# A decoder trunk in fp32: gated projections that begin with half of the rows, loads from two queues, and later sums for the first norm

## Chip, cores, metric

One Trainium2 chip, one core. The metric is device time of the whole program in microseconds, the median of several executions. Each run shown has also one profiled execution, and the tables below are of that one.

## What is computed

Two layers, each a half-step gated FFN, a mixer of three kinds of attention, and a second half-step gated FFN, on 256 tokens of width 1024; a norm stands ahead of each part and at the end.

```python
def _rmsnorm(x, g):
    y = x * lax.rsqrt(jnp.mean(x * x, axis=-1, keepdims=True) + RMS_EPS)
    return y * g

def _swiglu(x, w_gate, w_up, w_down):          # 1024 -> 2816 -> 1024
    return (jax.nn.silu(x @ w_gate) * (x @ w_up)) @ w_down

for l in range(DEPTH):                          # DEPTH = 2
    x = x + 0.5 * _swiglu(_rmsnorm(x, ffn1_norm[l]), ffn1_w_gate[l], ffn1_w_up[l], ffn1_w_down[l])
    h = _rmsnorm(x, mix_norm[l])
    ...                                         # out_a, out_b, out_c from h @ w_in[l]
    x = x + jnp.concatenate([out_a, out_b, out_c], axis=-1) @ w_out[l]
    x = x + 0.5 * _swiglu(_rmsnorm(x, ffn2_norm[l]), ffn2_w_gate[l], ffn2_w_up[l], ffn2_w_down[l])
return _rmsnorm(x, final_norm)
```

## The kernel before

Activations lie transposed: eight row tiles x[k] of 128 features by 256 tokens. All products are in fp32 by halves. A weight chunk of 128 x 1024 is loaded raw, ACT casts its high half (`whi`, line 152) and DVE subtracts to get the low half (`wlo`, line 153); an operand tile is likewise made of a high half, times the norm's gain, on ACT (line 229) and a low half on DVE (line 230). `mm2` (line 284) makes one pair of matmuls: the high weights times both halves of the operand (512 columns), then the low weights times the high half (256 columns).

In an FFN (line 302) the 2816 columns of gate and up go in 22 steps of 128. Column i needs two chunks: (i, 0) holds the weights of gate and up for rows 0 to 3, (i, 1) those for rows 4 to 7, so each chunk is eight pairs. The chunks are computed in the order (0, 0), (0, 1), (1, 0), (1, 1), (2, 0), (2, 1), and then column by column. A column needs two PSUM banks, of the tag "mm" (four banks), or "at" (four banks) for each third column. `next_w` hands out chunks in the order in which they are loaded and splits the chunk three further on, except at two places of the head, whose splits are made up for after `norm.column()`.

The norm's scale is applied late. `square` (line 233) takes the squares of two row tiles on ACT and adds them on GpSimd (lines 243, 247); `column` multiplies the sums by ones on TensorE (`pss`) and takes the power on GpSimd; `rms_row` turns the result into a row on TensorE (`prow`). Where this is done in the head of an FFN is said by `AT`: the column after pair 33, the row after pair 42 of 48. Then each column is evacuated (`add_halves`, line 295), scaled, put through Silu on ACT, multiplied, and split into halves for the down projection.

At the start of the program the SP queue issues, one after the other: the gains, row tile 0, the weights for it, row tiles 1 to 3, the weights for them, row tiles 4 to 7, the second chunk, and then further chunks (lines 175 to 186). GpSimd makes an identity, and TensorE runs 12 warm-up products on it (24 matmuls; line 217). Lines 710 to 718 make the operands of all eight row tiles and the halves of the first three chunks; the squares of the first norm come after the first two chunks of products. The order on each engine is that of a list scheduler, which follows the order of the program where inputs are ready; TensorE's order is the program's.

Of the kernel before, what the change touches and what calls it, by code (L numbers as in the profile page):

```python
# [10 lines left out]
F32 = mybir.dt.float32  # L11
F32R = mybir.dt.float32r
AF = mybir.ActivationFunctionType
OP = mybir.AluOpType

P = 128
# [3 lines left out]
DK = D // P  # L20
# [15 lines left out]
NDIST = 384  # L36
CH = DK * P
RAW, SPLIT_AHEAD = 5, 3
WARM = 12
AT = (0, 9)  # L40

FIRST = ((0, 1), (1, 4))

# [34 lines left out]
def tile_trunk(ctx, tc, xT, gains, kvg, sinks, table, onehot, wgu, wdn, winv, wins, wkv, wout, out):  # L78
# [47 lines left out]
    def room(i):  # L126
        raws[i] = wpool.tile([P, 2, CH], F32, tag="raw", name=f"raw{i}", bufs=RAW)
        return raws[i]
# [33 lines left out]
    def next_w(pieces=1, ahead=True):  # L162
        n = cursor[0]
        cursor[0] += 1
        split(n)
        if ahead:
            split(n + SPLIT_AHEAD, pieces)
        load(n + 2 * RAW - 1)
        return parts.pop(n)
# [2 lines left out]
    xs = act.tile([P, DK, T], F32, name="xs")  # L172
    x = [xs[:, k, :] for k in range(DK)]
    gain = const.tile([P, (3 * DEPTH + 1) * DK], F32, name="gain")
    nc.sync.dma_start(out=gain, in_=gains)
    room(0)
    for a, b in FIRST:
        nc.sync.dma_start(out=xs[:, a:b, :], in_=xT[:, a:b, :])
        nc.sync.dma_start(out=raws[0][:, 0, 2 * a * P:2 * b * P], in_=loads[0][:, 0, 2 * a * P:2 * b * P])
    nc.sync.dma_start(out=xs[:, DK // 2:, :], in_=xT[:, DK // 2:, :])  # L180
    nc.sync.dma_start(out=raws[0][:, 1, :], in_=loads[0][:, 1, :])
    room(1)
    for j in range(2):
        nc.sync.dma_start(out=raws[1][:, j, :], in_=loads[1][:, j, :])
    for n in range(2, RAW):
# [5 lines left out]
    nc.gpsimd.memset(ident, 0.0)  # L191
    nc.gpsimd.affine_select(out=ident, in_=ident, pattern=[[-1, P]], compare_op=OP.not_equal,
                            fill=1.0, base=0, channel_multiplier=1)
    ones = const.tile([P, 1], F32, name="ones")
    nc.vector.memset(ones, 1.0)
    mhalf = const.tile([P, 2], F32, name="mhalf")
    nc.vector.memset(mhalf, -0.5)

# [100 lines left out]
        nc.vector.tensor_add(a, p[:, :T], b)  # L299
        return a  # L300

    def ffn(norm, nxt, last=False, first=None, between=(), at=AT):
        hs, banks, ws = [], {}, {}

        def products(i, h, start=0, stop=DK):

            if start == 0:
                ws[0] = next_w(ahead=(i, h) not in ((1, 1), (2, 0)))
                if h == 0:
                    for m in range(2):  # L310
                        banks[i, m] = bank("pgu", "at" if i % 3 == 2 else "mm")
            whi, wlo = ws[0]
            for j in range(start, stop):
                k, m = h * DK // 2 + j // 2, j % 2
                c = slice(j * P, (j + 1) * P)
                mm2(banks[i, m], whi[:, c], wlo[:, c], xx[k], k == 0, k == DK - 1)


        products(0, 0)
        products(0, 1)  # L320
        if first:
            first()
        products(1, 0)
        products(1, 1)
        for n in range(2 * DK):
            products(2, n // DK, n % DK, n % DK + 1)
            if n == at[0]:
                col = norm.column()
                for m in range(2):
                    split(cursor[0] + SPLIT_AHEAD - 2 + m)  # L330
            if n == at[1]:
                row = rms_row(col)
        for i in range(FK):
            if i in between:
                between[i]()
            if i > 2:
                products(i, 0)
                products(i, 1)
            g, u = add_halves(banks.pop((i, 0)), "A"), add_halves(banks.pop((i, 1)), "C")
            t = tmp.tile([P, T], F32, tag="A", name="t")  # L340
            nc.vector.tensor_mul(t, g, row)
            s = tmp.tile([P, T], F32, tag="B", name="s")
            nc.scalar.activation(s, t, AF.Silu)  # L343
            sr = tmp.tile([P, T], F32, tag="B", name="sr")
            nc.gpsimd.tensor_mul(sr, s, row)  # L345
            h = tmp.tile([P, T], F32, tag="h", name="h", bufs=2)
            nc.vector.tensor_mul(h, sr, u)  # L347
            hs.append(act.tile([P, 2, T], F32R, tag=("hh", "hl")[i % 2], name=f"h{i}", bufs=FK // 2))
            nc.scalar.copy(hs[i][:, 0, :], h)  # L349
            nc.vector.tensor_sub(hs[i][:, 1, :], h, f(hs[i][:, 0, :]))  # L350
        for k in range(DK):
            p = bank("pdn")
            for kk in range(FK):
                j = (k * FK + kk) % DK
                if j == 0:
                    whi, wlo = next_w()
                c = slice(j * P, (j + 1) * P)
                mm2(p, whi[:, c], wlo[:, c], hs[kk], kk == 0, kk == FK - 1)
            if last and k:
                turn(k - 1)  # L360
            nc.vector.scalar_tensor_tensor(x[k], p[:, T:], 0.5, x[k], op0=OP.mult, op1=OP.add)
            residual(k, k + 1, p[:, None, :T], 0.5, nxt, last)
            nxt.square(k, last)
            if last:
                ys[k] = tmp.tile([P, T], F32, tag="A", name="y")
                nc.scalar.activation(ys[k], x[k], AF.Copy, scale=nxt.g(k))
# [342 lines left out]

    norm = Norm(0)  # L710
    parts[0], parts[1] = halves_of(0), halves_of(1)
    for k in range(DK):
        norm.operands(k)
        if k < DK // 2:
            split_part(0, 2 * k * P, 2 * (k + 1) * P)
        elif k % 2:
            split_part(1, (k - 5) * 2 * P, (k - 3) * 2 * P)
    split(2)
    start = norm

    def first_squares():
        for k in range(DK):
            start.square(k, after=start.ops[0])

    for l in range(DEPTH):
        nxt = Norm(3 * l + 1)
        ffn(norm, nxt, first=first_squares if l == 0 else None, between={3: load_bias, 6: make_bias} if l == 0 else {})
        norm, nxt = nxt, Norm(3 * l + 2)
        mix(l, norm, nxt)
        norm, nxt = nxt, Norm(3 * l + 3)  # L730
        ffn(norm, nxt, last=l == DEPTH - 1)
        norm = nxt
# [34 lines left out]
def _layout(x, rel_bias_table, ffn1_norm, ffn1_w_gate, ffn1_w_up, ffn1_w_down, mix_norm, w_in, attn_sinks,  # L767
            kv_norm_c, w_kv_up_c, w_out, ffn2_norm, ffn2_w_gate, ffn2_w_up, ffn2_w_down, final_norm):
    def cols(w, tiles):

        r = _rows(w)
        *a, p, k, n = r.shape
        return np.moveaxis(r.reshape(*a, p, k, tiles, n // tiles), -2, -4)

    g = np.stack([v for l in range(DEPTH) for v in (ffn1_norm[l], mix_norm[l], ffn2_norm[l])] + [final_norm])
    gu, dn = [], []
    for l in range(DEPTH):
        for wg, wu, wd in ((ffn1_w_gate, ffn1_w_up, ffn1_w_down), (ffn2_w_gate, ffn2_w_up, ffn2_w_down)):
            c = np.stack([cols(wg[l], FK), cols(wu[l], FK)], axis=3).reshape(FK, P, 2, DK * P)
            gu.append(np.moveaxis(c, 2, 1).reshape(2 * FK, P, DK * P))  # L780
            c = cols(wd[l], DK).reshape(DK, P, FK, P).transpose(0, 2, 1, 3).reshape(FK, DK, P, P)
            dn.append(np.moveaxis(c, 1, 2).reshape(FK, P, DK * P))
    order = [c for _, hs in STAT for h in hs for c in range(h, h + HD)]
    vcol = list(range(_VA, _VA + 128)) + list(range(_VB, _VB + 256)) + list(range(_WI, _WI + 4))
    rv = _rows(w_in[:, :, vcol])
    winv = np.moveaxis(rv.reshape(DEPTH, P, 4, 2 * VCOLS), 2, 1)
    wins = cols(w_in[:, :, order], NST).reshape(DEPTH, NST, P, DK * P)
    wkv = np.concatenate([w_kv_up_c[:, :, :HD], w_kv_up_c[:, :, :HD], w_kv_up_c[:, :, HD:]], axis=2)
    wo = w_out.reshape(DEPTH, NH, HD, D)[:, HEADS].reshape(DEPTH, DK, P, D)
    last = wo[:, -LASTK:].reshape(DEPTH, LASTK, P, DK, P).transpose(0, 3, 1, 2, 4).reshape(DEPTH, LASTK, DK, P, P)  # L790
    wo[:, -LASTK:] = last.transpose(0, 1, 3, 2, 4).reshape(DEPTH, LASTK, P, D)
    return {
        "xT": np.moveaxis(x[0].T.reshape(DK, P, T), 0, 1),
        "gains": np.moveaxis(g.reshape(-1, DK, P), 2, 0).reshape(P, -1),
        "kvg": kv_norm_c.T,
        "sinks": attn_sinks[:, HEADS[:NA]].reshape(1, -1),
        "table": rel_bias_table,
        "onehot": _distances(),
        "wgu": np.stack(gu),
        "wdn": np.stack(dn),  # L800
        "winv": winv,
        "wins": wins,
        "wkv": wkv,
        "wout": wo,
    }
# [17 lines left out]
```

## Time and profile before

| | |
|---|---|
| median of 3 runs | 972.26 us (971.99 to 973.49) |
| profiled execution, whole | 975.89 us |
| its span, first to last instruction | 974.1 us |
| TensorE busy | 955.7 us, 98% of the span |
| VectorE (DVE) busy | 706.3 us, 73% |
| ScalarE (ACT) busy | 533.8 us, 55% |
| GpSimd (POOL) busy | 161.6 us, 17% |
| DMA | 174.41 MB, mean 179 GB/s |

Times of instructions are from the start of the span. A row of the timeline gives start, duration, engine (PE is TensorE; a q behind the name is the engine's queue), line, operation, the tile written and those read, and in brackets the idle time before it with what ended it. Ends of matmuls are modelled, so distances are better taken from start to start.

### The profile page before, as it was taken

What the parts mean: (1) busy time and instruction counts of PE and PEld (TensorE: products, weight loads), DVE (VectorE), ACT (ScalarE), POOL (GpSimd) and SP (SyncE); (2) the same over time, 40 slices, a digit from 0 to 9 for tenths busy, and PEclk for the clock granted to TensorE, in tenths of its full rate; (3) what the DMA queues carried; (4) which work ended last, traced back from release to release, by engine and by line L of the source; (5) the groups of instructions that cost most, each with busy time, mean ns of one, the idle gap of its engine ahead of it and who ended that gap; (6) DMA issues with size and microseconds to landing.
All of it is one profiled execution on the core that took longest, in us unless ns stands there. A gap on an engine that the chain in (4) does not pass through costs nothing.

```text
span 974.1 us, 15598 instructions
## 1 busy us (share of the span) xinstructions
PE 955.7 (98%) x5924; PEld 846.5 (87%) x5924; DVE 706.3 (73%) x1307; ACT 533.8 (55%) x960; POOL 161.6 (17%) x148
## 2 busy tenths in 40 slices
PE   8999999999999999999999999999999999999996
PEld 6888888898899888888888888889988988888885
DVE  5787775668956877776668777666797678777552
ACT  6655554444656665654446555544465576555442
POOL 3221110110102221110012121001002042121001
PEclk9999999999999999999999999999999999999998
DMA  8688545553334555555555555545433455556511
GB/s 335 217 302 297 199 173 184 181 187 112 121 131 135 196 192 197 189 175 190 196 173 181 208 174 197 192 158 210 152 131 95 166 173 179 209 174 194 196 44 43
DMA packets 47575, 174.41 MB, mean 179 GB/s; under 512 B 3291, under 2 KB 5867, under 8 KB 47372
## 3 DMA queue, kind: packets, MB, share of 16 engines
q1 hardware_dynamic: 47212, 172.90, 51.8%
q8 instruction: 46, 0.75, 0.3%
q10 hardware_dynamic: 288, 0.52, 0.1%
q14 instruction: 29, 0.24, 0.1%
HBM read 172.34 MB, written 4.22 MB: 181 GB/s over the span
## 4 chain that ended last, share of the span: by engine, by line
PE 89%; DVE 4%; issue 4%; ACT 1%; POOL 1%; DMA 1%; SPq 0%; POOLq 0%; DVEq 0%; ACTq 0%
PE pgu L210 49%; PE pdn L210 22%; PE pp L210 6%; PE pwo L210 5%; PE pv L210 2%; PE po L210 1%; PE psc L210 1%; PE pt L213 1%; DVE wlo L153 1%; POOL ss L243 1%; DVE acc L494 1%; ACT whi L152 1%; DMA raw<-wgu 1%; DVE m L493 1%; DVE sb L565 0%
## 5 line engine op out<-in xcount | busy, mean ns | idle before, releaser
L210 PE MATMUL pgu<-xx,whi 128*128 128x512 f32 x1408 | 494.6, 396 | 2.0 <-ACT whi L152 2.0
L153 DVE TENSOR_TENSOR wlo<-raw,whi 128x1024 fp32r<-128x1024 f32 (+2 forms) x322 | 392.9, 1223 | 135.2 <-ACT whi L152 127.7
L152 ACT CAST whi<-raw 128x1024 fp32r<-128x1024 f32 (+2 forms) x322 | 332.7, 1034 | 257.6 <-PE pdn L210 110.1
L210 PE MATMUL pgu<-xx,wlo 128*128 128x256 f32 x1408 | 395.0, 281 | 0.2 <-DVE wlo L153 0.2
L210 PEld LDWEIGHTS pgu<-xx,whi 128*128 128x128 f32 x1408 | 264.0, 188 | 64.4 <-ACT whi L152 2.7
L210 PEld LDWEIGHTS pgu<-xx,wlo 128*128 128x128 f32 x1408 | 266.1, 189 | 0.8 <-DVE wlo L153 0.8
L210 PE MATMUL pdn<-h,whi 128*128 128x512 f32 x704 | 248.2, 397 | 0.0
L210 PE MATMUL pdn<-h,wlo 128*128 128x256 f32 x704 | 197.6, 281 | 0.0
L210 PEld LDWEIGHTS pdn<-h,whi 128*128 128x128 f32 x704 | 132.1, 188 | 31.3
L345 POOL TENSOR_TENSOR sr<-s,rrow 128x256 f32<-128x256 f32 x88 | 98.1, 1115 | 355.1 <-ACT s L343 354.8
L210 PEld LDWEIGHTS pdn<-h,wlo 128*128 128x128 f32 x704 | 133.1, 189 | 0.0
L297 ACT COPY b<-pgu 128x256 f32<-128x256 f32 x176 | 65.3, 372 | 80.8 <-PE pgu L210 80.8
L210 PE MATMUL pp<-xx,whi 128*128 128x256 f32 x480 | 92.1, 292 | 0.0
L299 DVE TENSOR_TENSOR a<-pgu,b 128x256 f32<-128x256 f32 x176 | 73.5, 419 | 25.3 <-ACT b L297 24.8
L210 PEld LDWEIGHTS pp<-xx,whi 128*128 128x128 f32 x480 | 75.4, 194 | 2.7 <-issue 1.7
L210 PE MATMUL pp<-xx,wlo 128*128 128x256 f32 x240 | 68.2, 284 | 0.0
L347 DVE TENSOR_TENSOR h<-sr,a 128x256 f32<-128x256 f32 x88 | 37.4, 425 | 29.2 <-POOL sr L345 28.8
L210 PE MATMUL pwo<-ohl,whi 128*128 128x256 f32 x256 | 47.6, 287 | 0.0
L210 PEld LDWEIGHTS pp<-xx,wlo 128*128 128x128 f32 x240 | 46.5, 194 | 0.0
L349 ACT CAST h<-h 128x256 fp32r<-128x256 f32 x88 | 35.3, 401 | 18.6 <-DVE h L347 18.6
L243 POOL TENSOR_TENSOR ss<-sq 128x512 f32<-128x512 f32 x7 | 10.2, 1458 | 196.4 <-ACT sq L238 196.4
L571 ACT ACTIVATE e<-sb,nm 128x256 f32<-128x256 f32 x64 | 28.4, 446 | 25.8 <-DVE nm L565 25.8
(98 smaller groups left out, 692.1 us busy)
## 6 DMA issues: line engine op xcount, KB each, us to landing
raw<-wgu SPq DMA_DIRECT2D x86, 1024.0 KB, 5.0
raw<-wdn SPq DMA_DIRECT2D x44, 1024.0 KB, 4.9
raw<-wins SPq DMA_DIRECT2D x14, 1024.0 KB, 5.0
raw<-wout SPq DMA_DIRECT2D x8, 1024.0 KB, 4.9
raw<-winv SPq DMA_DIRECT2D x4, 776.0 KB, 4.2
w<-u SPq DMA_DIRECT2D x1, 3072.0 KB, 14.1
bias<-w SPq DMA_DIRECT2D x1, 2048.0 KB, 9.3
raw<-wgu SPq DMA_DIRECT2D x3, 512.0 KB, 7.9
```

The lines of the kernel that those rows point to most:

```text
L152: ops = (nc.scalar.copy(hi[:, a:b], raw(n, a, b)), nc.vector.tensor_sub(lo[:, a:b], raw(n, a, b), f(hi[:, a:b])))
L153: nc.vector.tensor_sub(lo[:, a:b], raw(n, a, b), f(hi[:, a:b])))
L210: in_order(nc.tensor.matmul(*a, **kw))
L213: in_order(nc.tensor.transpose(*a))
L243: nc.gpsimd.tensor_add(s, self.sums[0], sq)
L297: nc.scalar.copy(b, p[:, T:])
L299: nc.vector.tensor_add(a, p[:, :T], b)
L345: nc.gpsimd.tensor_mul(sr, s, row)
L347: nc.vector.tensor_mul(h, sr, u)
L349: nc.scalar.copy(hs[i][:, 0, :], h)
L493: nc.vector.max(out=m8, in_=acc[:, cs])
L571: nc.scalar.activation(e[:, cs], sb[:, cs], AF.Exp, scale=-1.0, bias=nms[i][:, b, m:m + 1], accum_out=dens[i][:, b, m:m + 1])
```

## The change

Chunks of the first three columns are computed and laid out in memory in the order (0, 0), (1, 0), (2, 0), (0, 1), (1, 1), (2, 1), in all four FFNs. The first column's banks are evacuated after the fourth of them. In the first FFN the norm's column stands after pair 38 and its row after pair 48; in the others after 33 and 42, as before. At the start, rows 0 to 3 go out from SP, and the weights for them, the gains, and rows 4 to 7 from ACT's queue. A Silu of one element on ACT, between the first and the second weight load, brings the function table. The operands of rows 4 to 7 come after the split of the second chunk, and the squares of the first norm are set among the operands and splits, ahead of the FFN. There are 9 warm-up products in place of 12.

```diff
-WARM = 12
-AT = (0, 9)
+WARM = 9
+HEAD = ((0, 0), (1, 0), (2, 0), (0, 1), (1, 1), (2, 1))
+AT = ((4, 0), (5, 1))
+AT0 = ((4, 5), (5, 7))
...
-    nc.sync.dma_start(out=gain, in_=gains)
+    ones = const.tile([P, 1], F32, name="ones")
+    nc.vector.memset(ones, 1.0)
     room(0)
-    for a, b in FIRST:
+    for i, (a, b) in enumerate(FIRST):
         nc.sync.dma_start(out=xs[:, a:b, :], in_=xT[:, a:b, :])
-        nc.sync.dma_start(out=raws[0][:, 0, 2 * a * P:2 * b * P], in_=loads[0][:, 0, 2 * a * P:2 * b * P])
-    nc.sync.dma_start(out=xs[:, DK // 2:, :], in_=xT[:, DK // 2:, :])
+        nc.scalar.dma_start(out=raws[0][:, 0, 2 * a * P:2 * b * P], in_=loads[0][:, 0, 2 * a * P:2 * b * P])
+        if i == 0:
+            nc.scalar.dma_start(out=gain, in_=gains)
+            nc.scalar.activation(tmp.tile([P, 1], F32, tag="first", name="first", bufs=1), ones, AF.Silu)
     nc.sync.dma_start(out=raws[0][:, 1, :], in_=loads[0][:, 1, :])
+    nc.scalar.dma_start(out=xs[:, DK // 2:, :], in_=xT[:, DK // 2:, :])
     room(1)
...
-        products(0, 0)
-        products(0, 1)
-        if first:
-            first()
-        products(1, 0)
-        products(1, 1)
-        for n in range(2 * DK):
-            products(2, n // DK, n % DK, n % DK + 1)
-            if n == at[0]:
-                col = norm.column()
-                for m in range(2):
-                    split(cursor[0] + SPLIT_AHEAD - 2 + m)
-            if n == at[1]:
-                row = rms_row(col)
+        done = {}
+        for n, (i, h) in enumerate(HEAD):
+            for j in range(DK):
+                products(i, h, n not in (at[0][0] - 1, at[0][0]), j, j + 1)
+                if (n, j) == at[0]:
+                    col = norm.column()
+                    for m in range(2):
+                        split(cursor[0] + SPLIT_AHEAD - 2 + m)
+                if (n, j) == at[1]:
+                    row = rms_row(col)
+            if (i, h) == (0, 1):
+                done[0] = gate_and_up(0)
...
-            g, u = add_halves(banks.pop((i, 0)), "A"), add_halves(banks.pop((i, 1)), "C")
+            g, u = done.pop(i, None) or gate_and_up(i)
...
-    for k in range(DK):
+    for k in range(DK // 2):
         norm.operands(k)
-        if k < DK // 2:
-            split_part(0, 2 * k * P, 2 * (k + 1) * P)
-        elif k % 2:
-            split_part(1, (k - 5) * 2 * P, (k - 3) * 2 * P)
-    split(2)
-    start = norm
-
-    def first_squares():
-        for k in range(DK):
-            start.square(k, after=start.ops[0])
+        split_part(0, 2 * k * P, 2 * (k + 1) * P)
+    for c in range(0, CH, CH // 2):
+        split_part(1, c, c + CH // 2)
+    for k in range(DK // 2, DK):
+        norm.operands(k)
+        if k == 5:
+            split(2)
+            norm.square(1)
+            norm.square(3)
+    split(3)
+    norm.square(5)
+    norm.square(7)
```

## Rows read from the trace of the kernel before

**Rows 1.** Profile page, chain that ended last: shares of the span by engine.
```profile
PE 89%; DVE 4%; issue 4%; ACT 1%; POOL 1%; DMA 1%; SPq 0%; POOLq 0%; DVEq 0%; ACTq 0%
```

**Rows 2.** Chain of waits in order of time: start us, us, what.
```profile
46.86 90.65 PE pgu L210 x512
...
303.98 11.66 PE pgu L210 x66
```

**Rows 3.** Timeline of TensorE, start of the program: warm-ups, pairs of chunks, first norm.
```profile
1.36 5.40 PE L210 MATMUL warm<-ident 128*128 128x128 f32 x24 [1.36 <-POOL ident L192]
...
8.93 0.51 PE L210 MATMUL pgu<-xx,whi 128*128 128x512 f32 x1 [1.47 <-ACT whi L152]
...
12.06 0.49 PE L210 MATMUL pgu<-xx,whi 128*128 128x512 f32 x1 [0.55 <-ACT whi L152]
...
15.45 0.39 PE L210 MATMUL pgu<-xx,whi 128*128 128x512 f32 x1
...
20.99 0.39 PE L210 MATMUL pgu<-xx,whi 128*128 128x512 f32 x1
...
22.69 0.61 PE L210 MATMUL pss<-ones,fold 128*128 128x1 f32 x4 [1.18 <-POOL fold L247]
...
28.67 0.39 PE L210 MATMUL pgu<-xx,whi 128*128 128x512 f32 x1
```

**Rows 4.** Timeline of SP's queue: issues of row tiles 1 to 3 and their weights.
```profile
2.12 0.43 SPq L178 DMA_DIRECT2D xs<-xT  x1
2.59 0.43 SPq L179 DMA_DIRECT2D raw<-wgu  x1
```

**Rows 5.** DMA issues: queue, count, KB each, median us to landing.
```profile
raw<-wgu SPq DMA_DIRECT2D x1, 384.0 KB, 5.9
...
out<-y ACTq DMA_DIRECT2D x2, 256.0 KB, 3.3
out<-y SPq DMA_DIRECT2D x2, 256.0 KB, 3.5
```

**Rows 6.** Stretches: us, engines' busy time, PEclk, DMA share, GB/s (last two).
```profile
2.00:3.00 1.00, 1.00 (x6) 1.00 (x6) 0.00 (x0) 0.00 (x0) 0.00 (x0) 1.00 0.50 140
...
5.00:6.00 1.00, 1.00 (x6) 1.00 (x6) 0.41 (x2) 0.84 (x3) 0.00 (x0) 1.00 0.61 126
6.00:7.00 1.00, 1.00 (x7) 0.96 (x7) 0.41 (x2) 0.00 (x0) 0.00 (x0) 1.00 0.98 372
```

**Rows 7.** Timeline of ACT: table load, operands, casts of weights, squares.
```profile
3.75 1.28 ACT L229 ACT_TABLE_LOAD   x1 [3.75 <-DMA xs<-xT]
...
8.47 0.71 ACT L152 CAST whi<-raw 128x256 fp32r<-128x256 f32 x2
...
9.80 1.71 ACT L229 ACTIVATE xx<-xs,gain 128x256 fp32r<-128x256 f32 x4
11.41 1.12 ACT L152 CAST whi<-raw 128x512 fp32r<-128x512 f32 x2
...
12.97 1.03 ACT L152 CAST whi<-raw 128x1024 fp32r<-128x1024 f32 x1
...
16.45 1.15 ACT L238 ACTIVATE sq<-xs 128x512 f32<-128x512 f32 x2 [0.97 <-POOL ss L243]
```

**Rows 8.** Timeline of DVE: low halves of a whole chunk.
```profile
14.04 1.23 DVE L153 TENSOR_TENSOR wlo<-raw,whi 128x1024 fp32r<-128x1024 f32 x1 [0.70 <-ACT whi L152]
15.52 1.98 DVE L153 TENSOR_TENSOR wlo<-raw,whi 128x1024 fp32r<-128x1024 f32 x1 [0.25 <-ACT whi L152]
```

**Rows 9.** Timeline of GpSimd: sums of the first norm's squares.
```profile
14.62 1.80 POOL L243 TENSOR_TENSOR ss<-sq 128x512 f32<-128x512 f32 x1 [13.31 <-ACT sq L238]
...
17.16 3.80 POOL L243 TENSOR_TENSOR ss<-ss,sq 128x512 f32<-128x512 f32 x2 [0.74 <-ACT sq L238]
21.04 1.59 POOL L247 TENSOR_TENSOR fold<-ss 128x256 f32<-128x256 f32 x1
```

**Rows 10.** Stretch in the first mixer, columns as in Rows 6.
```profile
238.50:242.00 3.50, 3.50 (x18) 3.50 (x18) 3.50 (x16) 2.22 (x9) 0.00 (x0) 0.52 0.51 200
```

More of the change, by code (lines that the diff above doesn't have):

```diff
@@ L193, in tile_trunk @@
                             fill=1.0, base=0, channel_multiplier=1)
-    ones = const.tile([P, 1], F32, name="ones")
-    nc.vector.memset(ones, 1.0)
     mhalf = const.tile([P, 2], F32, name="mhalf")
@@ L300, in add_halves, with ffn, products @@
         return a
-    def ffn(norm, nxt, last=False, first=None, between=(), at=AT):
+    def ffn(norm, nxt, last=False, between=(), at=AT):
         hs, banks, ws = [], {}, {}
-        def products(i, h, start=0, stop=DK):
-            if start == 0:
-                ws[0] = next_w(ahead=(i, h) not in ((1, 1), (2, 0)))
+        def products(i, h, ahead=True, begin=0, end=DK):
+            if begin == 0:
+                ws[0] = next_w(ahead=ahead)
                 if h == 0:
@@ L312, in products @@
             whi, wlo = ws[0]
-            for j in range(start, stop):
+            for j in range(begin, end):
                 k, m = h * DK // 2 + j // 2, j % 2
@@ L316, in products, with gate_and_up @@
                 mm2(banks[i, m], whi[:, c], wlo[:, c], xx[k], k == 0, k == DK - 1)
-        products(0, 0)
-        products(0, 1)
-        if first:
-            first()
-        products(1, 0)
-        products(1, 1)
-        for n in range(2 * DK):
-            products(2, n // DK, n % DK, n % DK + 1)
-            if n == at[0]:
-                col = norm.column()
-                for m in range(2):
-                    split(cursor[0] + SPLIT_AHEAD - 2 + m)
-            if n == at[1]:
-                row = rms_row(col)
+        def gate_and_up(i):
+            p = [banks.pop((i, m)) for m in range(2)]
+            return add_halves(p[0], "A"), add_halves(p[1], "C")
+        done = {}
[10 more added lines that the diff above has]
+                done[0] = gate_and_up(0)
         for i in range(FK):
@@ L711, in tile_trunk @@
     parts[0], parts[1] = halves_of(0), halves_of(1)
-    for k in range(DK):
+    for k in range(DK // 2):
         norm.operands(k)
-        if k < DK // 2:
-            split_part(0, 2 * k * P, 2 * (k + 1) * P)
-        elif k % 2:
-            split_part(1, (k - 5) * 2 * P, (k - 3) * 2 * P)
-    split(2)
-    start = norm
-    def first_squares():
-        for k in range(DK):
-            start.square(k, after=start.ops[0])
+        split_part(0, 2 * k * P, 2 * (k + 1) * P)
[10 more added lines that the diff above has]
+    norm.square(7)
     for l in range(DEPTH):
         nxt = Norm(3 * l + 1)
-        ffn(norm, nxt, first=first_squares if l == 0 else None, between={3: load_bias, 6: make_bias} if l == 0 else {})
+        ffn(norm, nxt, between={3: load_bias, 6: make_bias} if l == 0 else {}, at=AT if l else AT0)
         norm, nxt = nxt, Norm(3 * l + 2)
@@ L779, in _layout @@
             c = np.stack([cols(wg[l], FK), cols(wu[l], FK)], axis=3).reshape(FK, P, 2, DK * P)
-            gu.append(np.moveaxis(c, 2, 1).reshape(2 * FK, P, DK * P))
+            c = np.moveaxis(c, 2, 1).reshape(2 * FK, P, DK * P)
+            gu.append(np.concatenate([c[[2 * i + h for i, h in HEAD]], c[len(HEAD):]]))
             c = cols(wd[l], DK).reshape(DK, P, FK, P).transpose(0, 2, 1, 3).reshape(FK, DK, P, P)
```

## The prediction

> **What bounds the kernel now.** I read the chain of waits first: TensorE holds 89% of it [rows 1], so only an edit that lets TensorE start sooner or wait less moves the end. Then I looked for places where it waits. In the chain it runs for 90.65 us at a stretch in the first FFN [rows 2], and 33 product pairs follow the mixer's last products without a gap [rows 2]; the list of waits by engine names none for TensorE in the head of the second, third or fourth FFN. So the new order of chunks, which is used in all four FFNs, can win nothing in three of them. What is left is the start of the first FFN, and the rest of this is about its first 29 us.
>
> There I follow the start of each group of eight pairs on TensorE. One pair (a 512-column product with the high half of the weights, a 256-column one with the low half) takes 0.346 us undisturbed: the groups that start at 15.45 and 20.99 are sixteen pairs apart [rows 3]. The reader should see four places where TensorE loses time after its first two pairs [rows 3]:
> - it restarts at 8.93, released by the cast of weights that landed at 8.45: those bytes were issued at 2.59 [rows 4] and took 5.86, which the view rounds to 5.9 [rows 5]. I call this landing, the later one of the rows 1 to 3 and of the weights for them, L. The next six pairs would take 2.08 from 8.93, that is until 11.01, but the next group starts only at 12.06: 1.05 lost;
> - that group takes 3.39 to the next start at 15.45, where 2.77 would do: 0.62 lost;
> - after one pair of the fifth group (20.99 to 21.34) the norm's product pss waits until 22.69 for the last GpSimd sum: 1.35 lost.
> Together 3.0 us after L. The fourth FFN group of columns, from which TensorE never waits again, starts at 28.67, so L + 20.2.
>
> **The change, part by part.** *Loads.* Now seven loads stand in one queue, 0.47 us from issue to issue (2.12 to 2.59) [rows 4]. The DMA engines are half idle at first (share 0.50 and 140 GB/s from 2 to 3 us) and full later (372 GB/s from 6 to 7) [rows 6]. After the change the activation rows go out in the first two SP slots and the weights in ACT's first and third: rows 1 to 3 at about 1.2 where it was 2.12, the weights for them at about 1.65 where it was 2.59. Both are some 0.93 earlier; with the time to landing that these weights have now (5.86 [rows 5]) L becomes 7.5. Nothing in the trace shows two queues loaded at the start, so I bound L from both sides. The low end: between 5 and 6 us the engines moved only 126 GB/s [rows 6]; the 1052 KB up to these weights (28, twice 128, twice 384) at 372 GB/s take 2.9 us, and counted from 2.0, where the engines began, that is 4.9, with some 0.5 until it is signalled 5.4. The high end: the table load of 1.28 us [rows 7] stands on ACT between the first and the second weight load; if the issue waits until it has run, it goes at about 3.0 and L is 8.9. I take 7.5, since it keeps a measured landing time and moves only the issue.
>
> The Trainium skill ("DMA: Bandwidth & Descriptors", section "Issuing engines are not separate DMA queues") says that issuing from several engines saves only the issue time, as all transfers run on the same 16 DMA engines. This speaks against a gain in bandwidth; by it the term is the 0.93 of issue slots and the low end of L falls away. No run here shows it.
>
> *Table load and warm-ups.* The 1.28 us of table load leave the place ahead of the first operand [rows 7]. The first two pairs are then ready before 5 us, and the nine warm-ups end near 5.3 (24 matmuls took 5.40 [rows 3], 18 take 4.05, from 1.36). I count nothing for it: the third pair waits for L anyway. The cover is L itself; only if L fell below about 5.5 would the warm-ups set the pace. The later Silu table load goes too; it stands where TensorE does not wait.
>
> *Order of chunks, from L on.* ACT must make for each of the three rows an operand (0.43, from 1.71 for four) and a weight cast (0.36, from 0.71 for two) [rows 7]. Third pair: L + 0.48 as now, when the rows land ahead of the weights and the operand is done; L + 1.0, when both land together; I take L + 0.75. Pace over three rows on ACT is 0.79 a row against 0.69 on TensorE, 0.3 lost. The next chunk, (1, 0), needs no new operand, where the present order put four operands (1.71) ahead of its casts. Two half casts (1.12 [rows 7]) end at L + 3.5, DVE 0.65 behind: 0.1 lost instead of the larger part of 1.05 + 0.62. Chunk (2, 0): two operands to L + 4.4, a full cast of 1.03 to L + 5.4, its low half 1.23 on DVE [rows 8] to L + 6.65; TensorE arrives at about L + 6.2, runs the first high product, and loses 0.2. Chunk (0, 1): two squares (1.15), two operands, a cast: L + 8.4; the low half is there 1.23 to 1.98 later [rows 8] (the longer value stands beside a GpSimd sum, and the first sum now runs there): L + 9.65 to 10.4 against an arrival at 9.2, the first high product again going ahead: 0.2 to 1.0 lost, I take 0.55, midway. The casts for chunks (1, 1) and (2, 1) come after two more squares, ready by L + 12.2 and L + 13.8, ahead of TensorE.
>
> *Sums later.* The four GpSimd steps take 1.80 + 3.80 (two) + 1.59 = 7.2 us [rows 9]. They begin after the second square, L + 6.5, and end at about L + 14.2. The column is now asked for after 38 pairs in place of 33, at L + 14.4 to 15.0: the 1.35 go to zero, with a margin of a few tenths only. If it failed by 0.4, that would be the price. The row of factors is asked for at the 48th pair in place of the 42nd; its chain (pss, then POOL's power) has ten pairs, 3.46 us, as against nine now, so it is not late. What is queued behind is the first column's multiply and Silu, 2.1 us later in TensorE's count; the next banks on which TensorE depends are those of columns 1 and 2, asked for 16 and 32 pairs later. Evacuating column 0 early (two ACT copies, two DVE adds) sits in the slack after the casts. I count nothing for either.
>
> *Other FFNs.* Bank needs come 8 pairs earlier, 2.8 us, and the mixer's or down projection's last banks are free by then; the column and row keep their places (33 and 42). Zero, with 0.2 either way.
>
> **Sum.** Earlier L 0.95; losses 3.0 become 0.3 + 0.1 + 0.2 + 0.55 = 1.15, so 1.85 less; the start after L is 0.27 later. 0.95 + 1.85 - 0.27 = 2.5, rounded to 2.6 for the warm-ups and table load which I left at zero. The profiled execution took 975.89 around its span of 974.1; it should become 973.3. The median of the runs is 972.26, 3.6 below the profiled one; I carry the same difference over: 969.7.
>
> **Rivals.** In all of them the gain is 1.6 plus (8.45 - L), near enough.
> - *The landing is better than its issue slot.* L 5.4 to 6.6: the holes in the DMA engines between 2 and 6 us [rows 6] come from too little issued, and close. For it: share 0.50 at 2 us. Against it: from 4 to 6 us seven loads had already been issued and the rate was still low. Gain 3.4 to 4.6, time 967.7 to 968.9.
> - *The weights wait behind the table load, or the low rate persists and halves are shared with the chunks that SP sends behind.* L 8.0 to 9.5; gain 0.5 to 2.0, time about 971. For it: ACT is in program order. Against: an issue is work of ACT's queue, and the load, of its engine. If the table were loaded twice (the change then not doing what it says), the result would fall here too.
> - *First come, first served, slower.* If ACT's second weight load goes out at 3.0, after the table load, SP has by then sent chunks 1, 2 and 3, 512 KB each (one each 0.47 us [rows 4]). If the engines serve in order of arrival, 1536 KB at 372 to 410 GB/s stand ahead, 4.0 us: L is 8.45 + 4.0 = 12.4, a loss of 2.4, time 974.7. It decides from L = 10 on. Against it: at the very end two queues work side by side, and their 256 KB land in 3.3 and 3.5 us [rows 5], so neither was put behind.
> - *The clock.* Fewer warm-ups, then a wait for L. The granted clock was 0.52, the lower of its two levels of 1.2 and 2.4 GHz, from 238.5 to 242.0, in the first mixer [rows 10]. One such fall costs 3.5 x 0.48 = 1.7 us: time 971.4. The present gap of 1.47 us before 8.93 brought none that the rows show.
>
> The Trainium skill (same page, section "Queues, rings and completion order") has each DMA engine go round between the queues that have work, packet by packet. By that rule the slower rival does not happen; the equal landings at the end agree.
>
> **How the numbers follow.** What can be told from no change here is 0.2%, 1.94 us. Forecast, L from 6.6 to 8.0 (968.9 to 970.3): 0.42. Better landing: 0.20. Later landing, second table load: 0.22. First come, first served and other mishaps to the slower side: 0.10. Clock: 0.06. Faster by over 0.2%: 0.42, 0.20, less the forecast's edge: 0.60. Slower by over 0.2%: 0.11, nearly all the first-come case. The rest, 0.29, is within. The range reaches from the better landing, with 0.3 off for the other FFNs, 967.4, to the end of the later landing, 972.2; it leaves out the slower rival.
>
> **What would show it.** Right: the third pair starts near 8.2 (now 8.93), pss finds its sum ready, the fourth column starts near 26.1 (now 28.67), and nothing after it differs. Wrong: weights for rows 1 to 3 that land after 9; a wait at (0, 1) above 1 us for the low half; a pss that still waits for GpSimd; a gap in one of the other FFNs' heads.

## The result and the profile after

The changed kernel took 981.6 us (median of 4 runs, 980.5 to 983.7) against 972.1 us (4 runs, 968.3 to 973.5): the ratio is 1.0105, with a 95% interval from 1.0083 to 1.0126. It is 9.5 us slower where 2.5 us faster was forecast. The profiled execution took 980.91 around a span of 979.1.

TensorE at the start, from its timeline (start us, us, operation, count, in brackets the idle time ahead and what ended it); it answers to [rows 3]:

```profile
1.36 3.93 PE L217 MATMUL warm<-ident 128*128 128x128 f32 x18 [1.36 <-POOL ident L201]
7.43 0.47 PE L217 MATMUL pgu<-xx,whi 128*128 128x512 f32 x1 [2.15 <-DVE xx L237]
...
9.47 0.80 PE L217 MATMUL pgu<-xx,whi 128*128 128x512 f32 x1 [1.05 <-ACT whi L156]
10.07 0.45 PE L217 MATMUL pgu<-xx,wlo 128*128 128x256 f32 x1
10.31 0.63 PE L217 MATMUL pgu<-xx,whi 128*128 128x512 f32 x1
...
24.83 0.50 PE L217 MATMUL pss<-ones,fold 128*128 128x1 f32 x4
...
28.89 0.48 PE L217 MATMUL pgu<-xx,whi 128*128 128x512 f32 x1
```

The third pair starts at 9.47 (8.93 before), the norm's product pss runs without a wait (1.35 before), and the fourth column starts at 28.89, where it was 28.67. The waits that [rows 3] show behind the third pair are gone, and still nothing is won there. The stretches say why (us, busy time and count of PE, PEld, DVE, ACT, POOL, then granted clock, DMA share, GB/s):

```profile
4.90:8.20 3.30, 1.16 (x8) 0.79 (x6) 1.22 (x3) 1.21 (x3) 0.00 (x0) 1.00 0.99 381
8.30:15.00 6.70, 5.65 (x18) 4.68 (x18) 5.24 (x10) 5.99 (x14) 0.25 (x1) 0.50 1.03 416
15.20:22.00 6.80, 6.80 (x41) 5.91 (x40) 6.22 (x5) 5.20 (x7) 5.67 (x4) 1.00 1.02 409
```

From 8.3 to 15.0 the granted clock is 0.50, the level of 1.2 GHz, and a pair takes 0.64 us (10.31 to 10.95) instead of 0.35. The kernel before had 1.00 in the same stretch. Ahead of the fall TensorE had been idle for 2.15 us, until 7.43.

What ACT does at the start (its queue's issues and its own work; answers to [rows 4] and [rows 7]):

```profile
1.17 0.45 ACTq L186 DMA_DIRECT2D gain<-gains  x1
1.65 1.28 ACT L188 ACT_TABLE_LOAD   x1 [1.65 <-PEq L824]
1.72 0.39 ACTq L184 DMA_DIRECT2D raw<-wgu  x1
...
6.26 0.51 ACT L236 ACTIVATE xx<-xs,gain 128x256 fp32r<-128x256 f32 x1 [3.11 <-DMA gain<-gains]
...
9.02 0.40 ACT L156 CAST whi<-raw 128x256 fp32r<-128x256 f32 x1 [1.54 <-DMA raw<-wgu]
```

The gains, issued at 1.17, hold up the first operand until 6.26. The weights for row tiles 1 to 3 are issued at 1.72, at once and not behind the table load, but land 7.28 us later.

The larger part of the loss is elsewhere. First the long pieces of the chain of waits of the changed kernel (start us, us, what, count), which answer to [rows 2]:

```profile
47.16 90.65 PE pgu L217 x512
...
302.81 11.66 PE pgu L217 x66
...
318.42 109.53 PE pgu L217 x620
427.95 62.18 PE pdn L217 x352
490.13 11.66 PE pgu L217 x66
...
505.57 109.53 PE pgu L217 x620
615.10 62.18 PE pdn L217 x352
...
780.12 11.66 PE pgu L217 x66
...
795.73 109.54 PE pgu L217 x620
```

And the same view of the kernel before, where two FFNs differ from the one ahead of them:

```profile
319.59 109.54 PE pgu L210 x620
429.13 62.19 PE pdn L210 x352
491.32 11.66 PE pgu L210 x66
...
506.82 107.48 PE pgu L210 x620
614.30 61.01 PE pdn L210 x352
...
778.14 11.66 PE pgu L210 x66
...
793.70 107.47 PE pgu L210 x620
```

The same 620 products (310 pairs), without a wait, take 107.48 or 109.53 us, that is 346.7 or 353.3 ns a pair; the 352 of the down projection take 61.01 or 62.18. So TensorE has two paces at the full granted clock. Before, the third and fourth FFN ran at the short one; after, none does. A whole FFN, 528 pairs, costs 3.5 us more at the long pace. The start of each stretch, before and after, gives the account of the two executions:

| point | before | after | difference |
|---|---|---|---|
| fourth column of the first FFN | 28.67 | 28.89 | +0.2 |
| second FFN | 303.98 | 302.81 | -1.2 |
| third FFN | 491.32 | 490.13 | -1.2 |
| fourth FFN | 778.14 | 780.12 | +2.0 |
| its down projection | 901.17 | 905.27 | +4.1 |
| span | 974.1 | 979.1 | +5.0 |

The -1.4 ahead of the second FFN is not the change's doing: the kernel before had half the granted clock in its first mixer [rows 10], which costs 1.7 by the estimate in the prediction, and this execution of the changed kernel had the full clock there. The execution of before that was profiled is 3.8 us above its median, that of after 0.7 below, which makes the 5.0 a 9.5 in the medians. The pace can differ from one execution of a kernel to the next; below, both paces in one trace are added up as the *long-pace time*: what each pair's start to the next start takes above 346.7 ns, summed over all pairs (7.6 us before, 13.3 after).

### The profile page after: what moved, and what is told of

The parts are those of the page before. It is cut to its first block, busy times and chain, and to the rows that moved or that the text cites. A ratio compares the mean times of both kernels' runs of the same rounds, so it can differ in the third digit from the quotient of the medians.

```text
span 979.1 us, 15577 instructions
## 1 busy us (share of the span) xinstructions
PE 960.2 (98%) x5918; PEld 846.1 (86%) x5918; DVE 708.7 (72%) x1307; ACT 532.5 (54%) x960; POOL 161.0 (16%) x148
## 4 chain that ended last, share of the span: by engine, by line
PE 90%; DVE 4%; issue 3%; ACT 1%; DMA 1%; POOL 1%; ACTq 0%; POOLq 0%; DVEq 0%
PE pgu L217 51%; PE pdn L217 22%; PE pp L217 6%; PE pwo L217 5%; PE pv L217 2%; PE po L217 1%; PE psc L217 1%; PE pt L220 1%; DVE wlo L157 1%; DMA raw<-wgu 1%; DVE acc L503 1%; DVE m L502 1%; DVE sb L574 0%; ACT e L580 0%; ACT whi L156 0%
## 5 line engine op out<-in xcount | busy, mean ns | idle before, releaser
L217 PE MATMUL pgu<-xx,whi 128*128 128x512 f32 x1408 | 501.1, 400 | 3.2 <-DVE xx L237 2.1
```

The source lines that it names most:

```text
L217: in_order(nc.tensor.matmul(*a, **kw))
```

## The experiments

Medians are given with the ratio to the kernel before, run on the same chip (its median was 972.2 in the first set and 971.0 to 971.5 in the later ones).

**First set: which part of the change?** Two kernels alter the start and keep the rest, two split the change between the FFNs.

`e1_warm12`:
```
-WARM = 9
+WARM = 12
```


> The changed kernel with 12 warm-ups in place of 9, nothing else. Theory of the clock: in the changed kernel nine pairs at the start ran at 0.64 us each instead of 0.35, since TensorE had stood still ahead of them; with three more warm-ups the gap is filled for 1.3 us, the pairs run at the full clock, and the time falls by 2 to 2.5 us against the changed kernel (981.6 to about 979.3). Theory of the pace (later pairs take 353 ns on average where they took 347 in part of the kernel before): the stretch after 320 us is as in the changed kernel, so at most these 2.5 us come back. Theory of chance (the pace is drawn anew in each execution): executions scatter from 968 to 982.

Measured: 981.4, ratio 1.0094 (1.0074 to 1.0114). The clock falls later and for a shorter time (0.50 from 10.5 to 13.8), and the fourth column starts at 28.19, 0.7 earlier. The 2 to 2.5 us that the theory of the clock promised do not appear in the median. All later FFNs keep the long pace, long-pace time 13.4.

`e2_one_queue`: all first loads from SP, the gains first.
```
+    nc.sync.dma_start(out=gain, in_=gains)
...
-        nc.scalar.dma_start(out=raws[0][:, 0, 2 * a * P:2 * b * P], ...)
+        nc.sync.dma_start(out=raws[0][:, 0, 2 * a * P:2 * b * P], ...)
...
-    nc.scalar.dma_start(out=xs[:, DK // 2:, :], in_=xT[:, DK // 2:, :])
+    nc.sync.dma_start(out=xs[:, DK // 2:, :], in_=xT[:, DK // 2:, :])
```


> The changed kernel with all first loads again from SP's queue, the gains first; the early table load stays. Theory of the loads: the gains land at 2.5 us instead of 6.3 and the weights for rows 1 to 3 at or before 8.5 instead of 9.0; the first pair starts at 5.3 instead of 7.4, and the fourth column some 0.5 to 1 us earlier. Theory of the clock: the gap from the first two pairs to the third is then 2 us or more, and the low clock is met as before or for longer, so the time stays within 1 us of the changed kernel. Theory of the pace: nothing changes after 320 us; 980 to 982.

Measured: 982.1, ratio 1.0097 (1.0079 to 1.0115). The first pair starts at 5.22 instead of 7.43, so it was the place of the gains that had held it. The third starts at 9.69: ACT now waits for the row tiles until 8.04 and makes three operands before the first cast. The weights for them, issued at 2.59, took 6.4 us and landed at 9.0, as late as from two queues; at or before 8.5 was expected. TensorE is idle for 3.00 us ahead of it, and the granted clock is 0.50 from 9.8 to 13.2.

`e3_order_2to4`: the kernel before, with the new order of chunks and the early evacuation of column 0 in the second to fourth FFN alone (`head` is the old order in the first FFN, the new one in the others).
```
-    def ffn(norm, nxt, last=False, first=None, between=(), at=AT):
+    def ffn(norm, nxt, last=False, between=(), at=AT, head=HEAD, first=None):
...
+        for n, (i, h) in enumerate(head):
```


> The kernel before, with the new order of chunks (and the early evacuation of the first column) in the second, third and fourth FFN only; the start and the first FFN are those of before. Theory of the pace, set by the order: long pairs (353 ns) in all three, slower than before by about 6 to 7 us, 978 to 979. Theory of the start: within 1 us of before, 972. Theory of chance: anything from 968 to 979, and the trace shows short pairs in some FFN of the three.

`e4_first_only`: the changed kernel with the old order in the second to fourth FFN (`HEADED` holds for the first one only).
```
-        ffn(norm, nxt, last=l == DEPTH - 1)
+        ffn(norm, nxt, last=l == DEPTH - 1, head=HEAD if HEADED(2 * l + 1) else OLD)
```


> The changed kernel with the new order in the first FFN only; the second, third and fourth have the order of before. Theory of the pace, set by the order: short pairs return in the third and fourth FFN, 6 to 7 us faster than the changed kernel, 975. Theory of the start: as slow as the changed kernel, 981. Theory of chance: from 972 to 982, with no relation to the order.

Measured: the order in the later FFNs alone 974.5, ratio 1.0035 (1.0016 to 1.0054), with the third and fourth FFN at the short pace; the rest of the change without it 982.8, ratio 1.0111 (1.0092 to 1.013), with all later FFNs at the long one. So the order of chunks is not what makes the change slow: whatever sets the pace 500 us into the program comes with the edits at its start. But the order alone is not free either: the first of the two is 2.3 us above the kernel before, with an interval that lies above 1, and its runs lie in two groups, 973 to 975 and 977 to 980. What the order does there was not followed up.

**Second set: the start's timing, or places in SBUF?** One effect of those edits reaches to the end of the program: `ones` is now allocated ahead of the identity, and a one-column scratch tile (`first`) is new. Each takes 32 bytes of a partition. In the built programs the identity lies at 16896 before and 16928 after, and the scratch tiles are 32 bytes further on; some of them, the column that the row products load among them, also lie in another part of the scratch, since the new code allocates them in another order. The weights and the operands of gate and up have the same places; the operand of the down projection is a scratch tile and moves by the 32 bytes. In the FFNs the identity is used by the two small products that spread a norm's factors to a row (prow), two between 1056 large ones.

`a1_const_moved`, the kernel before with:
```
+    ones = const.tile([P, 1], F32, name="ones")
+    nc.vector.memset(ones, 1.0)
     nc.sync.dma_start(out=gain, in_=gains)
...
-    ones = const.tile([P, 1], F32, name="ones")
-    nc.vector.memset(ones, 1.0)
```


> The kernel before, with one thing changed: the constant column of ones is allocated and set early, as the change does, so that the identity that the row transposes multiply with lies 32 bytes further on. The traces so far show two paces of the pairs of products in the gated projections, 346.7 and 353.3 ns a pair, that hold from one break of the stream to the next; the third and fourth FFN run at the short one in the kernel before and at the long one in the changed kernel, and 528 pairs each make 3.5 us per FFN. Theory 'places' (the shifted operands of the small products at the breaks set the pace): the third and fourth FFN run at the long pace here, 7 us more, about 979. Theory 'start' (the fall of the granted clock or the other timing at the start sets it): 972, with the short pace in both.

`a2_tmp_moved`, the kernel before with:
```
+    nc.vector.memset(tmp.tile([P, 1], F32, tag="first", name="first", bufs=1), 0.0)
```


> The kernel before, with only a one-column scratch tile added, so that all scratch tiles (the folded sums and the column that the breaks' products read among them) lie 32 bytes further on, as in the changed kernel. Theory 'places', if it is these operands and not the identity: long pace in the third and fourth FFN, about 979. Theory 'start': 972. If the first kernel of this set shows the long pace and this one does not, it is the identity's place; the other way round, the scratch tiles'.

`a3_places_back`, the changed kernel with:
```
+    ident = const.tile([P, P], F32, name="ident")     # and kvgain, sink, nsink: ahead of ones
...
-            nc.scalar.activation(tmp.tile([P, 1], F32, tag="first", ...), ones, AF.Silu)
+            nc.scalar.activation(nsink[:, 0:1], ones, AF.Silu)
```


> The changed kernel, with the identity, the ones and the scratch tiles put back to the places that they have in the kernel before (the early Silu writes into a column of the sink tile that is filled later). Order, queues, warm-ups and sums are those of the change. Theory 'places': the third and fourth FFN return to the short pace, 981.6 - 7 = 975, and the start still shows half the granted clock from about 8.3 to 15 us. Theory 'start': 981 to 982 as the changed kernel.

`a4_extra_row`, the kernel before with:
```
+        for _ in range(2):
             for b in range(2):
                 transpose(p[:, b * P:(b + 1) * P], col[:, b:b + 1].to_broadcast([P, P]), ident)
```


> The kernel before, with the two transposes that spread a norm's row made twice in each place, so that the break in the stream at the row is longer by two small products (some 0.3 us each time at most, about 12 places of which those in the FFNs count four times). If the pace is set by where a break leaves the stream, some FFNs change pace: the second one, at the long pace before, could come out 3.5 us shorter, the third and fourth 3.5 us longer each. If the pace belongs to the FFN (its loads, its place in memory) and not to the break, all keep theirs and the time is 973 to 975.

Measured: constants moved 979.2, ratio 1.008 (1.0054 to 1.0106); scratch tiles moved 972.0, ratio 1.0008 (0.9989 to 1.0028); the changed kernel with these places put back 971.9, ratio 1.0002 (0.9985 to 1.0019); twice the row products 979.4, ratio 1.008 (1.005 to 1.0109). The chain of waits of the first, with nothing changed but where one tile is allocated and set, in the third and fourth FFN:

```profile
504.08 109.53 PE pgu L210 x620
613.61 62.18 PE pdn L210 x352
...
795.56 109.53 PE pgu L210 x620
```

and of the changed kernel with identity and ones at their old places and the scratch without the extra 32 bytes (its tiles still in the order of the change), all three later FFNs:

```profile
317.58 107.48 PE pgu L217 x620
425.06 61.01 PE pdn L217 x352
...
501.36 107.48 PE pgu L217 x620
608.84 61.01 PE pdn L217 x352
...
789.71 107.48 PE pgu L217 x620
```

Theory "places" holds in both directions, and theory "start" falls: this last kernel has the fall of the clock, longer idle times and all the rest of the change, and its long-pace time is 1.3 us instead of 13.3. In the other direction my 7 us more were 8. Doubling the row products changes the pace too (the fourth FFN is at the long one): 16 more products of 0.27 us, 4.3 us at the very most, cost 8. That speaks for these interruptions as the place where the pace is settled; the next set tests it.

**Third set: which products, and the clock.**

`c1_ident64`, the changed kernel with the identity 64 bytes beyond its place in the kernel before:
```
+    mhalf = const.tile([P, 2], F32, name="mhalf")
     ident = const.tile([P, P], F32, name="ident")
```


> The changed kernel, with one small constant tile allocated ahead of the identity instead of behind it, so that the identity lies 64 bytes beyond its place in the kernel before instead of 32 bytes; the ones, the scratch tiles and everything else keep the places of the changed kernel. Theory 'the identity at an odd multiple of 32 bytes': the long pace goes, some 6 us less, 972 to 976. Theory 'any other place than that of before' or 'the ones (moved with it in the earlier run) are the cause': no change, 981 to 982.

`c2_row_only`, the kernel before with a second identity (at 17440, 32 past a multiple of 512) for the row products:
```
+    ident2 = const.tile([P, P], F32, name="ident2")   # filled like ident
...
-            transpose(p[:, ...], col[:, b:b + 1].to_broadcast([P, P]), ident)
+            transpose(p[:, ...], col[:, b:b + 1].to_broadcast([P, P]), ident2)
```


> The kernel before, with a second identity at an odd multiple of 32 bytes, which only the 16 transposes that spread a norm's row (prow) multiply with; the warm-ups, the mixer's and the output's transposes keep the first one. Theory 'the row transposes at the breaks inside the FFNs decide the pace': 977 to 979, as with the identity itself moved. Theory 'the mixer's transposes, or the warm-ups': 971 to 972.

`c3_warm16`, `a3_places_back` with `WARM = 16`:

> The changed kernel with the places of before (972 with nine warm-ups), and 16 pairs of warm-up products instead of nine, so that TensorE has work from 1.4 us until about 8.7 us, shortly before the weights of row tiles 1 to 3 land at 9.0 to 9.3. If the fall of the granted clock at 8.3 to 8.8 us is due to the idle time ahead of it, it goes, and of the 6.8 us at half clock 2 to 3.4 us come back: 968.5 to 970, faster than the kernel before by about 2 us. If the clock falls whatever runs there, 972.

`c4_mix_only`, the kernel before with the second identity in the mixers' transposes:
```
-                    transpose(pt[:, n * P:(n + 1) * P], e[:, c * P:(c + 1) * P], ident)
+                    transpose(pt[:, n * P:(n + 1) * P], e[:, c * P:(c + 1) * P], ident2)
```


> The same second identity in the kernel before, used by the 96 transposes of the mixers alone. Theory 'row transposes': 971 to 972, no change. Theory 'the mixer's transposes decide (they are the last products ahead of the third FFN's stream)': 977 to 979. If neither this kernel nor the one with the rows alone is slower, the place acts through the warm-ups or through both together.

Measured: row products alone 978.2, ratio 1.0074 (1.005 to 1.0098); the mixers' transposes alone 972.1, ratio 1.0 (0.9986 to 1.0014). In the built programs of these two kernels every tile has the same place (the large tiles lie 512 bytes beyond the kernel before in both), so they differ only in which products read the second identity. So it is the row products, 16 of some 5900 on TensorE, and the chain of waits of the former shows all FFNs at the long pace:

```profile
319.84 109.54 PE pgu L214 x620
...
507.07 109.53 PE pgu L214 x620
616.60 62.18 PE pdn L214 x352
...
798.61 109.54 PE pgu L214 x620
```

They take no longer themselves: 270 to 273 ns each both before and after. The 64 bytes did not help, 983.4, ratio 1.0121 (1.0104 to 1.0138): my theory of an odd multiple of 32 bytes was wrong.

With 16 pairs of warm-ups the median is 969.4, ratio 0.999 (0.9969 to 1.0012). TensorE at its start:

```profile
1.36 6.05 PE L217 MATMUL warm<-ident 128*128 128x128 f32 x32 [1.36 <-POOL ident L201]
7.75 0.47 PE L217 MATMUL pgu<-xx,whi 128*128 128x512 f32 x1 [0.34 <-DVE xx L237]
...
9.36 0.49 PE L217 MATMUL pgu<-xx,whi 128*128 128x512 f32 x1 [0.63 <-ACT whi L156]
...
22.27 0.40 PE L217 MATMUL pgu<-xx,whi 128*128 128x512 f32 x1
...
22.88 0.61 PE L217 MATMUL pss<-ones,fold 128*128 128x1 f32 x4
...
27.10 0.48 PE L217 MATMUL pgu<-xx,whi 128*128 128x512 f32 x1
```

The idle times are 0.34 and 0.63, the granted clock stays at 1.00 up to the first mixer, and the fourth column starts at 27.10, 1.6 earlier than in the kernel before. From the third pair it takes 17.74 us to there, against 19.42 in the changed kernel and 19.40 in `a3_places_back`, which differs in the warm-ups alone: the half clock cost 1.7. The pair ahead of pss starts at 22.27, so pss could start at 22.62; it starts at 22.88. The chain of waits shows the last GpSimd sum just ahead of it:

```profile
21.23 1.61 POOL fold L254
22.88 0.61 PE pss L217 x4
```

At the full clock pss waits for GpSimd again, 0.3 us where it was 1.35. The execution that was profiled is this kernel's slowest (978.7); it has the long pace in three FFNs, so even this place does not always give the short one.

**Fourth set: which places?**

`d1_ident64_old`, the kernel before with `ones` and `mhalf` allocated ahead of the identity (64 bytes further on, at 16960):

> The kernel before with the two small constants allocated ahead of the identity, which lies 64 bytes further on; nothing else has another place, except those constants. Theory 'only the place of before gives the short pace in the third and fourth FFN': 977 to 980. Theory 'a multiple of 64 bytes is as good' (then the slow run with 64 bytes in the changed kernel had another reason): 971 to 972.

`d2_ones_only`, the kernel before with `mhalf` allocated ahead of `ones` (the ones 32 bytes further on):

> The kernel before with the identity at its place and only the column of ones moved by 32 bytes. If the ones (moving operand of the sums' products, three of the breaks) take part: 975 to 980. If the identity alone decides: 971 to 972.

`d3_warm16_tmp`, `c3_warm16` with the scratch tile `first` of the change:

> The changed kernel with 16 warm-up pairs and the identity and ones at the places of before, the scratch tiles 32 bytes further on as the change has them. If the identity's place is what matters, the long pace is as rare as with all places put back: 967 to 971, 1 to 4 us below the kernel before. If the scratch tiles (the column that the row transposes load as weights) matter too: 975 to 979.

`d4_ident512`, the kernel before with a spare tile of 512 bytes:
```
+    const.tile([P, P], F32, name="spare")
     ident = const.tile([P, P], F32, name="ident")
```


> The kernel before with a spare 512-byte tile ahead of the identity, so that it lies 512 bytes further on (as do the ones and all tiles behind it). Theory 'it is the place within 512 bytes or a smaller unit': 971 to 972 as before. Theory 'any other place is slow': 977 to 980.

Measured: identity 64 bytes on 977.7, ratio 1.006 (1.0041 to 1.008); ones alone 972.2, ratio 1.0008 (0.999 to 1.0026); 512 bytes on 972.1, ratio 1.0006 (0.9989 to 1.0022), here with all three later FFNs at the short pace (all tiles behind the identity move too, those of the large products among them):

```profile
319.27 107.48 PE pgu L211 x620
...
503.05 107.48 PE pgu L211 x620
...
789.98 107.48 PE pgu L211 x620
```

The scratch tiles moved beside 16 warm-up pairs gave 973.4, ratio 1.0025 (1.0007 to 1.0043), between my two expectations; its median is 4 us above `c3_warm16`, where moving them in the kernel before (`a2_tmp_moved`) had done nothing. Whether they matter stays open. All kernels together, by the place of the identity that the row products read:

| identity past a multiple of 512 bytes | start of the kernel before: median (long-pace time) | start of the change |
|---|---|---|
| 0 | before 971.5 (7.6), a2 972.0 (4.3), c4 972.1 (7.5), d2 972.2 (4.1), d4 972.1 (4.1), e3 974.5 (7.7) | a3 971.9 (1.3), c3 969.4 (10.1), d3 973.4 (9.2) |
| 32 | a1 979.2 (10.4), c2 978.2 (13.8) | after 981.6 (13.3), e1 981.4 (13.4), e2 982.1 (13.2), e4 982.8 (13.2) |
| 64 | d1 977.7 (9.8) | c1 983.4 (13.5) |

The median is of all runs, the long-pace time of one execution each. No kernel of the first line is above 974.5, none of the others below 977.6; only `a4_extra_row`, with other products at the break, does not fit a line (0 bytes, 979.4, 10.0). Shown is that the place decides how often the long pace comes, and that a multiple of 512 bytes is good at two places (16896 and 17408). It does not fix the pace of each FFN: at 0 the profiled execution of the kernel before has the long pace in two of four, at 32 the first FFN of `a1_const_moved` has the short one (its 512 products take 88.95 us, not 90.65), at 64 the third of `d1_ident64_old`. Why a place of 32 or 64 bytes more leaves the following stream slower was not found.

## Why the prediction was wrong, step by step

- **"Other FFNs: zero, with 0.2 either way"** is the step that failed. Its reason was right as far as it went: no wait appears there (66 products take 11.66 us in both chains), and the order of chunks wins nothing there (alone it loses 2.3, `e3_order_2to4`). But I looked for what the change does to the order and the waits in those FFNs, and not for what it does to the places of the tiles they use. The price is 5.7 us of long-pace time in the two profiles (13.3 - 7.6), 8 to 10 in medians (`a1_const_moved` against the kernel before; the changed kernel, 981.6, against itself with the places put back, 971.9). The trace of before had the warning: its second and third FFN do the same work in 109.54 and 107.48 us, without a wait. I read "no gap" and did not ask why the durations differ.
- **L** was mis-sized: 9.0, not 7.5, and 0.1 beyond the upper bound of 8.9; it fell into the rival "L 8.0 to 9.5". The issue came 0.87 earlier (1.72 against 2.59 [rows 4]) and not behind the table load, but the landing took 7.28 where I had kept 5.86. The DMA engines moved 381 GB/s from 4.9 to 8.2 us, 300 before: more is in flight ahead of and beside these weights. That the other transfers take this load's share is my reading, and the second queue is not needed for it: in `e2_one_queue`, all from SP, these weights took 6.4 and landed at 9.0 too. In the other nine kernels with the start of before they took 5.3 to 5.8, so the row that I read, 5.86, was at the long end. Why both starts of the change land later stays open. The sentence of the Trainium skill ("DMA: Bandwidth & Descriptors", "Issuing engines are not separate DMA queues") that several issuing engines save only the time of issuing gives the 0.93 of my term: here not even that was saved. The slower rival, a landing after 10, did not happen; the issue that it put at 3.0 went out at 1.72, so the order of service was not tested.
- **"I count nothing" for warm-ups and first pairs.** I had the first two pairs ready before 5 us; the gains, now second in ACT's queue, landed at 6.26, and the first pair started at 7.43 (6.50 before). It is true that the third pair waits for L anyway. But the idle time is not free: after 2.15 us of it ahead of the first pair, where the kernel before had its longest, 1.47, ahead of the third [rows 3], the granted clock fell to half. The cover that I named was the landing, and the price if it is not filled with work is 1.7.
- **The clock rival** was right in mechanism; that its price came out (1.7 a fall, 1.7 measured between `c3_warm16` and the changed kernel) is luck. I had counted 3.5 us at half clock; it was 6.7, of which TensorE stood idle for 1.05, and the slow pairs covered waits for operands and for pss that `c3_warm16` has. I gave the rival 0.06 since 1.47 us of idle time had brought no fall. Fewer warm-ups, later gains and a later landing all lengthen it; this should have weighed more.
- **Order of chunks** was right, **later sums** nearly so. From the third pair to the fourth column I expected 17.9 us (8.2 to 26.1); `c3_warm16`, where the clock holds, takes 17.74, and the kernel before 19.74 [rows 3]. The gain of 2.0 is near the 1.85 of my sum. "pss finds its sum ready" failed by 0.3: in the changed kernel the last GpSimd sum ended at 22.92 and pss came at 24.83, but only because the half clock had held TensorE up; in `c3_warm16` pss waits for the sum. The margin of a few tenths was not there.
- **The sum.** Of the 2.5 us, 1.6 are there when clock and places are mended, as the start of the fourth column in `c3_warm16` shows (27.10; 27.27 in `d3_warm16_tmp`, and 28.25 to 29.03 in the ten kernels with the start of before). L took 1.4 of the forecast (8.87 in that execution, not 7.5); 0.3 came back since the third pair starts 0.5 after L and not 0.75, and 0.15 with the order of chunks. In the median that is 969.4 against 971.5, which its interval (0.9969 to 1.0012) does not tell from no change. As the change was made, the half clock takes the gain back (28.89 against 28.67), and the pace adds the rest.

## What to carry to other kernels

Compare stretches of equal work in one trace with each other: where they have no waits and still differ, something sets a pace, and an edit far away can move it. An edit that allocates a tile, or moves an allocation, changes the place of everything behind it; keep the operands of small products that interrupt a long stream where they were, or put them on a multiple of 512 bytes (good at the two places tried here, for a reason not known), and look at the durations of the long stretches after every change. Idle time on TensorE ahead of a wait that is "there anyway" is to be filled with warm-up products up to the wait's end, or the granted clock may fall with it.

## What the runs showed of the hardware

- The stream of pairs (512 and 256 columns) has two paces at the granted clock of 1.00, 346.7 and 353.3 ns a pair, which hold for hundreds of pairs, as a rule until another product interrupts the stream. Two interrupting products of 270 ns can change it, and how often they leave the long one depends on the place of their moving operand in SBUF: at 0 and 512 bytes from the first place medians of 971.5 and 972.1, at 32 and 64 bytes 978.2 and 977.7. How the place does it is open.
- A small load on a second queue is not early because it is issued early: the gains landed 5.1 us after their issue at 1.17, behind the first weights in ACT's queue.
- In the starts looked at closely, the granted clock fell to 0.50 after idle times of 2.15 and 3.00 us, and also after 0.92 and 0.76 (`e1_warm12`); it held after 0.34 and 0.63, after 0.93 (`d3_warm16_tmp`), and in the kernel before after 1.47. No length of idle time that is safe can be read from that.
